# Conv b's taps behind a third of a slot, the root steps over two stages, and the third group's z gates in one slot

## The chip, the cores and the metric

The kernel runs on one core of a Trainium2 chip. The core has a matrix engine (TensorE, PE in the profile), a vector engine (VectorE, DVE), a scalar engine (ScalarE, ACT), a general engine (GpSimd, POOL) and a queue that only issues transfers (SyncE, SP). Each engine takes its instructions strictly in the order in which the program lists them, so an instruction that waits holds back everything listed behind it on its engine. The metric is the device time of one execution, in microseconds (us).

## The reference

One encoder layer is computed for a prompt of 1,024 tokens and a sample of 32 tokens; both are held together as 1,056 columns. A combined input projection of the 1,024 model features gives all branch inputs: a GLU pair and a gate for branch A, and z, x, B, C and dt for branch B, and three merge gates. In short:

```python
u = a_val * sigmoid(a_glu);  u = causal_dwconv31(u)            # conv a
out_a = (silu(layer_norm(u)) * silu(a_gate)) @ w_a_out
xbc = silu(causal_dwconv4(xbc))                                # conv b: 4 taps, 3,072 channels
xs, B, C = split(xbc);  dt = softplus(dt_raw + dt_bias)
y = ssd_scan(xs, dt, -exp(a_log), B, C, h0) + d_skip * xs      # 4 groups, state carried over the tokens
g = y * silu(z);  g = g * rsqrt(mean(g*g over a group) + eps)  # gated RMS norm, 4 groups
out_b = (g * gnorm_w) @ w_b_out
merged = sigmoid(g_a) * out_a + sigmoid(g_b) * out_b
x_new = layer_norm(alpha * x + merged @ w_out + sigmoid(g_p) * (p @ w_ple))
```

The kernel also returns the last rows of both convolutions and the final state of the scan.

## The kernel before

Channels lie on the 128 partitions, tokens along the free dimension. Every large product is done as three products of a high and a low part, so each weight tile is split by ScalarE (high part) and VectorE (low part, `wlo`).

**Slots.** The program is a list of slots written out by hand; a slot s is one or two output tiles of a product on TensorE. Slots 1 to 30 (`pair_slot`) compute pairs of tiles of the input projection. Slots 31 to 58 (S_CL on, the list `CLASSIC`) compute the 28 remaining tiles singly: z tiles, and for each of the scan's groups 1 to 3 the tiles B, C and four x tiles. Slots 59 to 70 are three quarters of the product of branch B, slots 71 to 78 branch A, 79 to 82 the last quarter, and then comes the output product. A single tile is 72 matmuls of 352 columns, in three token groups of 24, each evicted from PSUM by ScalarE (`evac`); three PSUM banks are used in turn.

**Stages of a slot** (`slot`, lines 314 to 351). Side work is put on a slot under a stage's name with `at(s, stage, fn)`. The stages run in this order: `ld0`, `ld`, `st`, `d0`, the split of the next weight tile, `a0`, `d1`; then the first token group; then `a1`; the second group; then `pm` and `a2`; the third group; then `d2`, `run_fill`, `pe` and `end`. Since each engine has its own queue, a stage says where in each engine's list the work stands.

**The scan** (`ssd_group`). Group g handles one chunk of 128 tokens per slot, from slots 32, 41, 50 and 59 on, nine chunks each. In the slot of a chunk: the decay tile L is loaded and computed on ScalarE (`decay`, `a2`), and TensorE transposes x and B at `pe`. One slot later: `prep` on VectorE (`a0`: two products into M and X, the mask, and L times it), `pe_o` on TensorE (`a1`: output from the carried state; it needs the PSUM bank of y free), `carry` on VectorE (`a2`: scales the carried state and y in PSUM), and `pe_d` on TensorE (`pe`: adds the chunk's own part into y and S, so it needs `carry` done). Two slots later: `update` (`d0`): ScalarE copies the state, and four VectorE operations read y out of PSUM. So TensorE's `pe_o` in a slot waits for `update` of the same slot, and `pe_d` at its end waits for `carry`.

**Conv b** (`conv_b`, lines 1147 to 1180). For the tile of slot s: `tap0` on ScalarE at slot s+1, `a0`; three taps on VectorE at s+1, `d2`, behind all else; SiLU on ScalarE first of all in slot s+2's `a0`. Tiles of slots 33 to 38, 42 to 47 and 52 to 57 are of this kind, so their taps stand in slots 34 to 39, 43 to 48 and 53 to 58.

**Conv a and the fill.** Conv a's 31 taps are a queue (`fill`) from which `run_fill` takes taps at a slot's end while a sum of estimated VectorE nanoseconds (`dve[0]`) is below a limit. The three taps of conv b also let up to two fills in between them. What is left at slot 37 is emptied there (`ca_flush`).

**z gates and roots** (`z_tile`, `rstd_chain`). For z tile j of group g with gate slot s: SiLU (if it comes from a pair slot) at `a1`, the gate product on VectorE at `d2` of s, its square on ScalarE at `a0` of s+1 and the sum over the four tiles on VectorE at `a1` of s+1. The group's last tile starts the root: column sums on TensorE at the end of s+1 (`stats`), the row copied by ScalarE at s+2 `a0`, moved through DRAM into 96 partitions (`move_row`, `d1`), square root and Newton step at s+2 `d2` (`root`: a square root on ScalarE and six small VectorE operations), and its store at s+2 `end`. The same chain serves conv a's layer norm with s = 53. The z gates of group 0 stand in slots 42 and 43, of group 1 in 51 and 52, of group 2 in 60 and 61, of group 3 in 71 and 72, two tiles in each.

Loads are issued from SP in the program's order, and from slot 31 on stores from POOL; both queues wait in place for what an entry needs. Buffers are handed out in the order in which the program frees them.

Of the kernel before, what the change touches and what calls it, by code (L numbers as in the profile page):

```python
# [36 lines left out]
F32 = mybir.dt.float32  # L37
# [4 lines left out]
P = 128  # L42
# [7 lines left out]
KA, KB = 31, 4  # L50
# [49 lines left out]
S_CL = 1 + len(PAIRS)  # L100
# [36 lines left out]
def emit(nc, tc, I, O, ctx):  # L137
    cpool = ctx.enter_context(tc.tile_pool(name="const", bufs=1))
# [35 lines left out]
    dve = [0.0]  # L174
# [15 lines left out]
    def tsc(out, a, s1, s2, op0, op1=None):  # L190
        dve[0] += 150 + 0.58 * width(out)
        if op1 is None:
            nc.vector.tensor_scalar(out, a, s1, None, op0)
        else:
            nc.vector.tensor_scalar(out, a, s1, s2, op0, op1)

    def act(out, a, f=AF.Copy, **kw):
        nc.scalar.activation(out, a, f, **kw)  # L198
# [21 lines left out]
    decb = cpool.tile([P, 32, 9], F32, name="decb")  # L220
    wsum = cpool.tile([P, 16], F32, name="wsum")
    small = cpool.tile([P, 64], F32, name="small")
    root_t = cpool.tile([P, 66], F32, name="root_t")
    nc.gpsimd.memset(ones, 1.0)
    nc.gpsimd.memset(epsb, EPS)
    nc.gpsimd.memset(ident, 0.0)
# [25 lines left out]
    busy = defaultdict(list)  # L252
    fill = deque()
    BREAK = object()

    def at(s, stage, fn, *a):
        todo[(s, stage)].append((fn, a))
# [6 lines left out]
    def run_fill(limit):  # L264
        while fill and dve[0] < limit:
            it = fill.popleft()
            if it is BREAK:
                break
            it()
# [44 lines left out]
    def slot(s, nm, nk, rhs, evac):  # L314

        dve_slot(11500.0 + sum(busy[s]))
        run(s, "ld0")
        w_load(s + 2)
        run(s, "ld")
        run(s, "st")  # L320
        run(s, "d0")
        w_split(s + 1)
        run(s, "a0")
        run(s, "d1")
        ws = wsplit.pop(s)
        if isinstance(ws, list):
            W = lambda q, i: ws[i // 4][q][:, i % 4 * P:i % 4 * P + P]
        else:
            W = lambda q, i: ws[q][:, i * P:i * P + P]
        spread = todo.pop((s, "dx"), [])  # L330
        n = 0
        for mi in range(nm):
            for g, (c0, c1) in enumerate(GR):
                ps = psum(bank())
                for k in range(nk):
                    xh, xl = rhs[k]
                    i = mi * nk + k
                    three(ps[:, :GN], W(0, i), W(1, i), xh[:, c0:c1], xl[:, c0:c1], k == 0, k == nk - 1)
                evac(mi, g, ps[:, :GN])
                for fn, a in spread[len(spread) * n // (3 * nm):len(spread) * (n + 1) // (3 * nm)]:  # L340
                    fn(*a)
                n += 1
                if n == nm:
                    run(s, "a1")
                elif n == 2 * nm:
                    run(s, "pm")
                    run(s, "a2")
        run(s, "d2")
        run_fill(11000.0 + sum(busy[s]))
        run(s, "pe")  # L350
        run(s, "end")

# [23 lines left out]
    def rstd_chain(get_v, scale, s, done):  # L376


        q = {}
        i = rows[0]  # L380
        rows[0] += 2
        o = 11 * 3 * (i // 2 % 2)
        sm = lambda k: root_t[:96, o + RC * k:o + RC * k + RC]

        def stats():
            q["v"] = get_v()
            q["ps"] = rows_pe(q["v"])

        def row():
            rows_copy(q["ps"], q["v"])  # L390

        def root():
            act(sm(1), sm(0), AF.Sqrt, bias=epsb[:96], scale=scale)
            tsc(sm(0), sm(0), scale, EPS, ALU.mult, ALU.add)
            nc.vector.reciprocal(sm(1), sm(1))
            newton(sm(1), sm(0), sm(2))

        def move_row():
            store(d_row[i:i + 1, :], q["v"][0:1, :])
            load(sm(0), d_row[i].rearrange("(p c) -> p c", p=96))  # L400
            tput(q["v"])

        def move_root():
            store(d_row[i + 1].rearrange("(p c) -> p c", p=96), sm(1))
            done(i + 1)

        at(s + 1, "pe", stats)
        at(s + 2, "a0", row)
        at(s + 2, "d1", move_row)
        at(s + 2, "d2", root)  # L410
        at(s + 2, "end", move_root)

    H = 32

# [722 lines left out]
    XSs, BCs, sgs, zst = {}, {}, {}, {}  # L1137
# [9 lines left out]
    def conv_b(ct, vin, s, done, stage="d2"):  # L1147

        acc = {}

        def tap0():
            acc[0] = tget((P, WB), F32, "cb")
            act(acc[0], vin[:, 0:WB], AF.Identity, bias=col(C_CBB + ct), scale=col(C_CBW + ct * KB))

        def tap(j):
            stt(acc[0], vin[:, j:j + WB], col(C_CBW + ct * KB + j), acc[0], ALU.mult, ALU.add)

        def out():
            store(O["conv_b"][ct * P:(ct + 1) * P, 0, :], vin[:, TP:TP + LB])
            store(O["conv_b"][ct * P:(ct + 1) * P, 1, :], vin[:, NT + LB:NT + 2 * LB], vin)  # L1160

        def silu():
            t = acc[0]
            act(t[:, :TP], t[:, :TP], AF.Silu)
            act(t[:, TP:NT], t[:, WB - TS:], AF.Silu)
            done(t)

        at(s + 1, "a0", tap0)

        def taps():  # L1170
            for j in range(1, KB):
                tap(j)
                if stage == "d2" and j < KB - 1 and fill and fill[0] is not BREAK and dve[0] < 9000.0:
                    fill.popleft()()
        at(s + 1, stage, taps)
        at(s + 2, "st", out)
        if s + 2 < S_CL:
            at(s + 2, "a2", silu)
        else:
            todo[(s + 2, "a0")].insert(0, (silu, ()))  # L1180

    def z_tile(g, j, zt, s):


        q = {"z": zt}

        def away():
            store(d_z[4 * g + j], zt, zt)

        def back():  # L1190
            q["z"] = tget(name="zt")
            load(q["z"], d_z[4 * g + j])

        def late_silu():
            act(q["z"], q["z"], AF.Silu)

        if s - cur[0] > 4:
            at(cur[0] + 1, "st", away)
            at(s, "ld", back)
        if cur[0] < S_CL:  # L1200
            at(s, "a1", late_silu)

        def gate():
            x = XSs[4 * g + j][:, :NT]
            tt(x, x, q["z"], ALU.mult)

        def square():
            act(q["z"], XSs[4 * g + j][:, :NT], AF.Square)

        def add():  # L1210
            if j == 0:
                zst[g] = q["z"]
            else:
                tt(zst[g], zst[g], q["z"], ALU.add)
                tput(q["z"])

        at(s, "d2", gate)
        at(s + 1, "a0", square)
        at(s + 1, "a1", add)

        def spill():
            store(d_yn[4 * g + j], XSs[4 * g + j][:, :NT], XSs[4 * g + j])

        at(s + 1, "a1", spill)
        if j == 3:
            rstd_chain(lambda: zst[g], 1.0 / 512, s, lambda i: yrow.update({g: i}))
# [310 lines left out]
    SSD0 = [S_CL + i for i in (1, 10, 19, 28)]  # L1537
# [67 lines left out]
    for i, (ta, tb) in enumerate(PAIRS):  # L1605
        s = i + 1
        cur[0] = s
        ba, bb = BIAS(2 * i), BIAS(2 * i + 1)
        (kind, n, _), (kb, nb, _) = ta, tb
        if kind == "glu":  # L1610
            sg = tget(name="sg")
            u = uin_tile(n)
            ca[n] = (u, sg)
            oa, ob = plain(sg), padded(u, LA, TP + 2 * LA)
            at(s + 1, "a0", lambda sg=sg: act(sg, sg, AF.Sigmoid))
            conv_a_ready(n, s + 1)
        elif kind in ("gate", "z"):
            ga, gb = tget(name="ga"), tget(name="gb")
            oa, ob = plain(ga), plain(gb)
            if kind == "z":  # L1620
                for z_, m in ((ga, n), (gb, nb)):
                    z_tile(m // 4, m % 4, z_, SSD0[m // 4] + (12 if m > 11 else 10) + m % 4 // 2)
            elif 8 <= n < 16:
                base_tiles(s, (ga, gb), (n - 8, nb - 8))
            else:
                at(s + 1, "st", gate_spill, ga, n)
                at(s + 1, "st", gate_spill, gb, nb)
        else:
            va, fa = vin_tile(kind, n)
            vb, fb = vin_tile(kb, nb)  # L1630
            oa, ob = padded(va, LB, TP + 2 * LB), padded(vb, LB, TP + 2 * LB)
            last = s == len(PAIRS)
            fa(s, *(() if last else ("a1",)))
            fb(s, *(() if last else ("a2",)))
        pair_slot(s, oa, ob, ba, bb)
# [14 lines left out]
    for ti, (kind, n, _) in enumerate(CLASSIC):  # L1650
# [7 lines left out]
        if kind == "z":  # L1658
# [2 lines left out]
            def evac(mi, g, ps, zt=zt, bias=bias):  # L1661
                act(zt[:, GR[g][0]:GR[g][1]], ps, AF.Silu, bias=bias)
            g_ = n // 4
            z_tile(g_, n % 4, zt, max(s + 1, SSD0[g_] + 10 + n % 4 // 2))
        elif kind == "glu":
            sg = sgs[n] = tget(name="sg")

# [249 lines left out]
```

## Time and profile before

| | |
|---|---|
| median of 3 runs | 1540.13 us (1538.54 to 1540.93) |
| the profiled execution | 1544.62 us; span 1542.8 us from the first to the last instruction |
| mean granted clock of TensorE | 0.989 |
| busy: TensorE, VectorE, ScalarE, GpSimd | 97%, 78%, 56%, 19% of the span |
| a slot with a chunk of the scan and no wait | 15.35 us (slot 47 from 913.80 to 929.15) |

Times in the trace are counted from the first instruction. Slots can be read off TensorE's rows: slot 31 begins at 659.45, slot 40 at 792.93, slot 50 at 964.17, slot 60 at 1127.19. A row of the timeline has its start, its length, the engine, the line, the operation, what it writes and reads, shapes, a count, and in brackets how long the engine had been idle before it and whose end released it. Names are the program's tiles with the buffer's letter: `cb` is a conv b tile, `vin` its input, `hT` the state of the scan, `L`, `M`, `X` the scan's operands, `cao` and `cae` conv a's two sums, `zt` a z tile, `root_t` the cells of the root, `cw` a weight tile that is being centred.

### The profile page before, as it was taken

The page shows a single profiled execution, that of the slowest core. Times are in us where ns is not written, and L with a number is a line of the kernel's source. Part 1 is how long each engine was busy: PE and PEld are TensorE (multiplying, and loading weights), DVE is VectorE, ACT ScalarE, POOL GpSimd, SP SyncE. Part 2 cuts the span into 40 slices and gives each one's busy share as a digit, 9 for nine tenths or more (in the row PEclk, how much of TensorE's full clock was granted, in tenths as well). Part 3 has the DMA queues.
Part 4 walks back from the last instruction along what each step waited for, and adds up shares of the span by engine and source line. Part 5 has one row for each costly group of instructions (what it writes and reads, how often), then busy time and mean ns, then how long its engine had stood idle before and what let it go on. Part 6 is the DMA issues. An engine that isn't in the chain of part 4 may idle for free.

```text
span 1542.8 us, 27648 instructions
## 1 busy us (share of the span) xinstructions
PE 1502.1 (97%) x10967; PEld 1455.5 (94%) x10967; DVE 1203.4 (78%) x1650; ACT 862.8 (56%) x1490; POOL 290.4 (19%) x445
## 2 busy tenths in 40 slices
PE   8999999999999999999999899998999999999997
PEld 7999999999999999998999788988988899999997
DVE  6669898989889899899875867666866887768554
ACT  7644635444444344576775677676877466634343
POOL 1343333333333333100001111001000000000000
PEclk9999999999999999999999999999999999999998
DMA  9987797988877686453548875764293545654132
GB/s 325 235 216 212 175 246 201 263 222 235 223 196 196 170 207 163 109 172 98 141 137 281 288 231 160 239 147 125 83 288 113 174 177 203 223 224 167 44 96 73
DMA packets 156306, 288.43 MB, mean 187 GB/s; under 512 B 26992, under 2 KB 83344, under 8 KB 156176
## 3 DMA queue, kind: packets, MB, share of 16 engines
q1 hardware_dynamic: 111936, 176.06, 36.0%
q0 software_dynamic: 44240, 110.61, 28.7%
q8 instruction: 86, 1.41, 0.4%
q14 instruction: 44, 0.36, 0.1%
HBM read 226.14 MB, written 60.46 MB: 186 GB/s over the span
## 4 chain that ended last, share of the span: by engine, by line
PE 84%; DVE 5%; ACT 4%; DMA 4%; issue 2%; SPq 1%; POOL 0%; ACTq 0%; DVEq 0%; POOLq 0%
PE ps L211 83%; SPq L201 1%; DVE cb_z L188 1%; ACT L198 1%; DMA cw_z<-in_wo 1%; DMA yraw_t<-d_yn 1%; PE ps L1058 1%; DMA cb_z<-d_base 1%; ACT L_t L198 1%; ACT L_z L198 1%; DMA w<-in_wdt 0%; DVE cae_u L188 0%; DMA E<-d_expa 0%; DMA s<-in_w 0%; DVE yraw_t L188 0%
## 5 line engine op out<-in xcount | busy, mean ns | idle before, releaser
L500 POOL DMA_DIRECT2D s<-in_w x150 | 132.3, 924 | 275.4 <-DMA s<-in_w 203.2
L188 DVE SCALAR_TENSOR_TENSOR cae_u<-uin_u,par,cae_u 128x1086 f32<-128x1086 f32 x120 | 161.2, 1343 | 0.0
L188 DVE SCALAR_TENSOR_TENSOR cao_u<-uin_u,par,cao_u 128x1086 f32<-128x1086 f32 x112 | 150.5, 1344 | 0.0
L184 DVE TENSOR_TENSOR wlo<-wraw,whi 128x1024 fp32r<-128x1024 f32 x53 | 64.8, 1223 | 44.4 <-ACT whi L198 44.3
L198 ACT ACT_TABLE_LOAD x73 | 93.7, 1283 | 2.9 <-DMA zt_t<-d_z 0.8
L198 ACT ACTIVATE whi<-wraw 128x1024 fp32r<-128x1024 f32 x53 | 55.9, 1054 | 42.1 <-PE ps L211 41.4
L495 POOL DMA_DIRECT2D r<-in_w x85 | 63.4, 799 | 28.2 <-DVE w_0l L184 20.3
L211 PE MATMUL ps<-t3h,w_4l 128*128 128x264 f32 x240 | 68.7, 286 | 0.0
L211 PE MATMUL ps<-n2h,w_2h 128*128 128x264 f32 x240 | 68.6, 286 | 0.0
L211 PE MATMUL ps<-t3l,w_4h 128*128 128x264 f32 x240 | 68.4, 285 | 0.0
L211 PE MATMUL ps<-t4h,w_6h 128*128 128x264 f32 x240 | 68.4, 285 | 0.0
L211 PE MATMUL ps<-n2l,w_2h 128*128 128x264 f32 x240 | 68.3, 285 | 0.0
L211 PE MATMUL ps<-t3h,w_4h 128*128 128x264 f32 x240 | 68.3, 285 | 0.0
L211 PE MATMUL ps<-n2h,w_2l 128*128 128x264 f32 x240 | 68.2, 284 | 0.0
L495 POOL DMA_DIRECT2D s<-in_w x84 | 48.2, 575 | 106.1 <-issue 28.2
L211 PE MATMUL ps<-t4l,w_6h 128*128 128x264 f32 x240 | 68.1, 284 | 0.0
L211 PE MATMUL ps<-t4h,w_6l 128*128 128x264 f32 x240 | 67.9, 283 | 0.0
L198 ACT ACTIVATE gb_t<-ps,par 128x528 f32<-128x528 f32 x32 | 22.5, 702 | 71.7 <-PE ps L211 67.6
L198 ACT ACTIVATE ga_t<-ps,par 128x528 f32<-128x528 f32 x38 | 26.7, 702 | 63.8 <-PE ps L211 63.8
L198 ACT ACTIVATE ps<-ps 128x528 f32<-128x528 f32 x28 | 16.7, 595 | 62.3 <-PE ps L211 62.3
L211 PEld LDWEIGHTS ps<-t3h,w_4h 128*128 128x128 f32 x240 | 45.3, 189 | 0.0
L211 PEld LDWEIGHTS ps<-n2l,w_2h 128*128 128x128 f32 x240 | 45.3, 189 | 0.0
(1174 smaller groups left out, 6062.0 us busy)
## 6 DMA issues: line engine op xcount, KB each, us to landing
s<-in_w POOLq DMA_DIRECT2D x234, 256.0 KB, 4.8
r<-in_w POOLq DMA_DIRECT2D x85, 256.0 KB, 5.1
wraw<-in_w SPq DMA_DIRECT2D x27, 512.0 KB, 8.2
wraw<-in_wb SPq DMA_DIRECT2D x16, 512.0 KB, 3.7
E<-d_expa SPq DMA_DIRECT2D x56, 128.0 KB, 7.9
d_gate<-ga_t SPq DMA_DIRECT2D x12, 528.0 KB, 6.3
L_z<-d_accp SPq DMA_DIRECT2D x12, 512.0 KB, 6.7
d_gate<-gb_t SPq DMA_DIRECT2D x10, 528.0 KB, 7.3
```

The source lines that it names most:

```text
L184: nc.vector.tensor_tensor(out, a, b, op)
L188: nc.vector.scalar_tensor_tensor(out, a, s, b, op0, op1)
L198: nc.scalar.activation(out, a, f, **kw)
L201: nc.sync.dma_start(dst, src)
L211: nc.tensor.matmul(out, l, r, start=start, stop=stop, skip_group_check=more)
L495: (nc.gpsimd if cur[0] else nc.sync).dma_start(t, pw_src(i, PARTS[n][0]))
L500: nc.gpsimd.dma_start(pr[i, n], pw_src(i, (PARTS[n] + ("12",))[k]), accum_op=ALU.add)
L1058: nc.tensor.transpose(pX[:nt, j * P:(j + 1) * P], XS[j][:, sl], ident)
```

## The change

Three edits go together.

1. **Taps.** For the tiles of slots 31 and later, the three conv b taps move from `d2` to `a1` of the same slot, and no fill is put between them. The limit of the fill in `slot` goes from 11,000 to 10,000.
2. **Roots.** The square root moves from `d2` of s+2 to `a0` of s+3, the VectorE steps become a function of their own (`steps`) at `a1` of s+3, and the store goes from `end` of s+2 to `a2` of s+3. Since two chains may now overlap, there are three sets of cells (99 columns).
3. **z gates.** All four z gates of group 2 stand in slot 60; the two that come from pair slots had been in slot 61. Their loads, SiLUs, squares and sums move with them by one slot, and so does the group's root chain, whose s becomes 60. The sum takes whichever tile comes first as its start.

```diff
-    root_t = cpool.tile([P, 66], F32, name="root_t")
+    root_t = cpool.tile([P, 99], F32, name="root_t")
@@ slot
-        run_fill(11000.0 + sum(busy[s]))
+        run_fill(10000.0 + sum(busy[s]))
@@ rstd_chain
-        o = 11 * 3 * (i // 2 % 2)
+        o = 11 * 3 * (i // 2 % 3)
...
         def root():
             act(sm(1), sm(0), AF.Sqrt, bias=epsb[:96], scale=scale)
+
+        def steps():
             tsc(sm(0), sm(0), scale, EPS, ALU.mult, ALU.add)
             nc.vector.reciprocal(sm(1), sm(1))
             newton(sm(1), sm(0), sm(2))
...
-        at(s + 2, "d2", root)
-        at(s + 2, "end", move_root)
+        at(s + 3, "a0", root)
+        at(s + 3, "a1", steps)
+        at(s + 3, "a2", move_root)
@@ conv_b
-                if stage == "d2" and j < KB - 1 and fill and fill[0] is not BREAK and dve[0] < 9000.0:
+                if s < S_CL and stage == "d2" and j < KB - 1 and fill and fill[0] is not BREAK and dve[0] < 9000.0:
                     fill.popleft()()
-        at(s + 1, stage, taps)
+        at(s + 1, "a1" if s >= S_CL else stage, taps)
@@ z_tile
-            if j == 0:
+            if g not in zst:
                 zst[g] = q["z"]
@@ the slots of the gates
-                    z_tile(m // 4, m % 4, z_, SSD0[m // 4] + (12 if m > 11 else 10) + m % 4 // 2)
+                    z_tile(m // 4, m % 4, z_, SSD0[m // 4] + (10, 10, 10, 12)[m // 4] + (m // 4 != 2) * (m % 4 // 2))
...
-            z_tile(g_, n % 4, zt, max(s + 1, SSD0[g_] + 10 + n % 4 // 2))
+            z_tile(g_, n % 4, zt, max(s + 1, SSD0[g_] + 10 + (g_ != 2) * (n % 4 // 2)))
```

## The prediction

> **What bounds the kernel now.** I read the page first. TensorE is busy nearly all the time, so time can be gained only where TensorE stands still or runs slowly.
>
> ```profile
> PE 1502.1 (97%) x10967; PEld 1455.5 (94%) x10967; DVE 1203.4 (78%) x1650; ACT 862.8 (56%) x1490; POOL 290.4 (19%) x445
> ```
>
> Next, the view of waits for TensorE alone: who was waited for, total, times, longest (us).
>
> ```profile
> PE ps L211 <- DVE cb_t L188: 11.6, 3, 6.0
> PE ps L211 <- DVE cb_z L188: 6.4, 3, 3.2
> ...
> PE ps L211 <- DVE cb_y L188: 2.0, 1, 2.0
> ```
>
> The three `cb` rows are 20.0 us in seven waits. Each is the scan's `pe_o` waiting for `update`, because VectorE came late into the slot. The view by windows of single slots (length, busy time of each engine, granted clock, DMA share, GB/s) places them: slots 34, 44, 46, an undisturbed one (47), 48, 55, 56, 60 and 64.
>
> ```profile
> 697.74:716.20 18.46, 16.47 (x115) 14.49 (x113) 18.39 (x22) 8.86 (x19) 0.74 (x2) 1.00 0.32 70
> 854.09:878.11 24.02, 18.00 (x114) 16.14 (x112) 23.25 (x29) 14.85 (x26) 5.40 (x10) 0.86 0.86 266
> 893.47:913.80 20.33, 17.14 (x108) 15.98 (x107) 17.51 (x27) 13.97 (x25) 5.97 (x11) 0.92 0.96 292
> 913.80:929.15 15.35, 15.35 (x108) 14.44 (x107) 10.40 (x16) 12.58 (x23) 1.07 (x2) 1.00 0.76 235
> 929.15:948.70 19.55, 17.18 (x109) 16.00 (x107) 18.61 (x25) 12.65 (x21) 3.26 (x6) 0.91 0.65 184
> 1041.52:1060.99 19.47, 17.15 (x108) 15.98 (x107) 10.87 (x21) 13.58 (x26) 2.13 (x4) 0.91 0.38 78
> 1060.99:1081.33 20.34, 17.16 (x108) 15.98 (x107) 15.86 (x29) 13.00 (x24) 3.07 (x6) 0.92 0.52 165
> 1127.19:1143.09 15.90, 14.96 (x101) 13.45 (x99) 9.80 (x13) 11.63 (x24) 1.62 (x3) 1.00 0.95 270
> 1190.48:1211.00 20.52, 17.32 (x108) 15.86 (x107) 14.11 (x30) 13.27 (x21) 0.53 (x1) 0.92 0.61 201
> ```
>
> Length less TensorE's busy time is its idle time: 2.0, 6.0, 3.2, 0, 2.4, 2.3, 3.2, 0.9 and 3.2 us. Where it was 2.3 us or more the granted clock fell to 0.86 to 0.92, and the same work took 1.8 us longer (17.14 against 15.35 in slot 46; 17.18, 17.15, 17.16 alike); at 2.0 us (slot 34) the clock stayed at 1.00. So a wait costs itself, and 1.8 us more from somewhere between 2.0 and 2.3 us on.
>
> The Trainium skill (TensorE: Matmul & The Clock Gate, Part 1) has the clock halved after an idle window of about 3.4 us; the trace disagrees, 2.3 us were enough here. By the page the new wait in slot 58 below would cost 1.8 us less, and the sum would be 1523 instead of 1525 us.
>
> **Part 1a, taps: slots 43 and 44.** The timeline there (VectorE, then ScalarE, then TensorE):
>
> ```profile
> 847.98 0.69 DVE L184 TENSOR_TENSOR ps<-ps,E 128x512 f32<-128x512 f32 x1
> 853.82 1.23 DVE L184 TENSOR_TENSOR cw_z<-cw_z,wsum 128x1024 f32<-128x1024 f32 x1 [5.15 <-DMA cw_z<-in_wo]
> 855.54 1.23 DVE L184 TENSOR_TENSOR cw_z<-cw_z,wsum 128x1024 f32<-128x1024 f32 x1 [0.49 <-DMA cw_z<-in_wo]
> ...
> 859.02 4.03 DVE L188 SCALAR_TENSOR_TENSOR cb_z<-vin_z,par,cb_z 128x1059 f32<-128x1059 f32 x3
> ...
> 870.94 0.69 DVE L184 TENSOR_TENSOR ps<-ps,E 128x512 f32<-128x512 f32 x1
> 847.94 1.27 ACT L198 ACTIVATE cb_z<-vin_z,par 128x1059 f32<-128x1059 f32 x1 [5.20 <-DMA out_ssm<-hT_z]
> 851.41 1.09 PE L211 MATMUL ps<-L_u,X 128*64 128x128 f32 x16
> 864.24 2.05 PE L211 MATMUL ps<-cb_t,hT_u 128*128 128x128 f32 x8 [6.02 <-DVE cb_t L188]
> 874.54 1.09 PE L211 MATMUL ps<-L_t,X 128*64 128x128 f32 x16
> ```
>
> VectorE finishes `carry` at 848.7, idles until 853.8 for a load, and the taps (4.03) come last, so `update` ends only at 864.2, where `pe_o` starts after 6.0 us. At `a1` the taps fill that hole, but stand ahead of `carry`. Tap 0 ends at 849.2 (its buffer waits for a store), so the taps end at 853.2 and `carry` (two operations of 0.69, started 0.6 apart: 1.3) at 854.5: `pe_d`, at 851.4 before, now waits 3.2 us. The rest of the slot starts 0.7 later, of which the second load's 0.5 is made up, so without the taps `update` ends at 864.2 less 4.0 plus 0.2, 860.4. From it to the end of slot 44's `carry` are 7.4 us (864.2 to 871.6), with the taps now inside 11.4: `pe_d` of slot 44 starts at 871.8 instead of 874.5. **Gain 2.8**; bounds: 0 if loads hold VectorE up, 7.8 if tap 0 comes early.
>
> **1b, slot 48.** The same lateness, with no such hole to lose: the taps leave the tail, `update` comes 4.0 earlier, more than the 2.4 waited. The slot returns to 15.35: **gain 4.2**, bounds 0 (loads then end last) and 4.2.
>
> **1c, new waits for `carry`.** In a quiet slot `carry` ends long before `pe_d`. Slot 38:
>
> ```profile
> 770.52 0.69 DVE L184 TENSOR_TENSOR ps<-ps,E 128x512 f32<-128x512 f32 x1
> 774.91 1.09 PE L211 MATMUL ps<-L_z,X 128*64 128x128 f32 x16
> ```
>
> 771.2 plus 4.0 is 775.2, 0.3 late. Doing this for all eighteen tap slots gives 0.3 in 38 and 39, 0.2 in 53, 0.4 in 57, nothing where no other work stands before `carry`: **loss 1.2** (0 to 3). The exception is slot 58, where branch B's first operands stand there too:
>
> ```profile
> 1104.87 1.31 DVE L188 SCALAR_TENSOR_TENSOR yraw_z<-yraw_z,par,yrb_u 128x1056 f32<-128x1056 f32 x1
> ...
> 1107.88 0.70 DVE L184 TENSOR_TENSOR ps<-ps,E 128x512 f32<-128x512 f32 x1
> 1109.35 1.09 PE L211 MATMUL ps<-L_y,X 128*64 128x128 f32 x16
> ```
>
> The taps go behind the 1104.87 row; `carry` moves from 1108.6 to 1112.6 and `pe_d` from 1109.4 (1109.8 after slot 57's 0.4): 2.9 us, over the bound of the clock: **loss 4.7** (1.8 to 6).
>
> **1d, the fill.** Followed by the cost lines 182 to 195, the lower limit drops one conv a tap (1.34) from slot 32 and adds one in 36; 33 to 35 keep eight, three and three. VectorE enters slot 34 1.26 us earlier, which comes off the 2.0 waited there: **gain 1.2** (0 to 2.0). The final addition moves to slot 37, whose VectorE has room.
>
> **Part 2, roots.** The square root stood behind the last eviction, so VectorE waited for it to the slot's end with the taps behind it. First the view of `root_t` for VectorE, then rows of slot 54 and ScalarE:
>
> ```profile
>   ACT root_t L198: 29.4, 4
> 1041.71 0.17 DVE L195 TENSOR_SCALAR root_t<-root_t 96x11 f32<-96x11 f32 x1 [10.66 <-ACT root_t L198]
> 1040.08 1.28 ACT L198 ACT_TABLE_LOAD   x1
> 1041.38 0.30 ACT L198 ACTIVATE root_t<-root_t,epsb 96x11 f32<-96x11 f32 x1
> 781.20 1.26 ACT L198 ACTIVATE cb_t<-vin_z,par 128x1059 f32<-128x1059 f32 x1
> ```
>
> These waits (slots 45, 54, 55, 63) make the long slots 46, 55, 56 and 64. VectorE now works on and does the steps (1.1) after `prep`. What is late next: the table load and root (1.6) go ahead of tap 0 on ScalarE. In slot 39 (start 777.58) tap 0 ends 4.9 into the slot; here 6.5 to 7.6, so `carry` (4.0 plus 1.3 behind it) ends 11.8 to 13.2 in, against `pe_d` at 12.7 (851.41 less 838.73): 0.3 lost in 46, none in 55, 0.5 in 56. **Gain** 4.7 + 4.1 + 4.4 = **13.2** (9 to 14.4), and in slot 64, without taps, 20.52 less 15.4: **5.1** (2 to 5.2). Behind the root on POOL stood the stores of the next slot; they leave earlier. The stores' readers follow slots later, and group 2's chain starts a slot sooner. The two roots of group 3 and the wider cells cost nothing: slots 72 to 75 have no wait.
>
> The Trainium skill (ScalarE: Activation LUTs, What ACT_TABLE_LOAD costs) adds a drain of about 1.38 us to each table load. The trace does not show it here: the root starts 0.02 us after its load. With it the three slots would lose some 4 us more: 1529.
>
> **Part 3, z gates.** Slot 60 gets two more loads, two SiLUs, two gates; slot 61 the squares and sums that 62 had. What that does is read from ScalarE's and TensorE's rows of slot 60:
>
> ```profile
> 1136.79 1.09 ACT L198 ACTIVATE y5h_t<-yraw_t 128x1056 fp32r<-128x1056 f32 x1 [4.23 <-DVE yraw_t L188]
> 1138.28 0.43 PE L211 MATMUL ps<-y0l_t,whi 128*128 128x352 f32 x1 [0.44 <-ACT acc_t L198]
> ```
>
> The load and the SiLUs themselves, in slot 61:
>
> ```profile
> 1150.43 1.28 ACT L198 ACT_TABLE_LOAD   x1
> 1151.73 2.06 ACT L198 ACTIVATE zt_t<-zt_t 128x1056 f32<-128x1056 f32 x2
> ```
>
> In slot 60 they come behind `y5h`, which is late already, and ahead of the eviction for which TensorE waits at 1138.28. Load and SiLUs (3.3) make 0.4 into 3.7 us, and the clock 1.8 more; slot 61 loses 0.4 to four squares and gains back its SiLUs' place. **Loss 5.5** (0 if ScalarE gets to them early, up to 8 as the two loads join a slot whose DMA share is 0.95).
>
> **The sum.** 2.8 + 4.2 + 13.2 + 5.1 + 1.2 = 26.5 gained, 1.2 + 4.7 + 5.5 = 11.4 lost, net 15.1. The profiled execution took 1544.62 us (span 1542.8), 4.5 above the median; 1544.6 less 15.1 is 1529.5, against the median of 1540.1 **1525 us**.
>
> **Rivals.** (A) The new waits of slots 58 and 60 don't arise or stay under the clock's bound: 1540.1 less 25.3 is 1515. For it: slot 58's is only 0.6 over the bound; against: both follow from fixed queue orders. (B) Loads end last once the waits are gone: the gains of 44, 46 and 48 (11.7) don't come, 1537. For it: DMA shares 0.86 and 0.96 there; against: in 47 the loads kept pace, and POOL's stores spread better. (C) Slower: tap 0 comes so late that in all of 43 to 48 and 53 to 58 `pe_d` waits for `carry` over the bound, which begins where tap 0 ends later than 9.6 us into the slot (12.7 + 2.2 less 5.3). Each costs 4.1: eleven slots beside 58 take 45 from a net 15: 1570. Slot 43 shows it can happen (10.5); the others' 4.9 speaks against. (D) The change only shifts waits: VectorE, 17.5 to 23 us busy in 44, 46 and 48, stays the bound and TensorE stands as long at `pe_d` as before at `pe_o`: 1540. Against: its long idle before the roots. (E) The table load holds ScalarE twice its 1.28: 1.3 more in 46, 55 and 56, 1529.
>
> **Chances.** Forecast 0.44, A 0.20, B 0.14, C 0.08, D 0.08, E 0.06. About 0.2% (3 us) is what a measurement can tell. Faster: forecast, A, E and most of B, 0.83; same 0.09 (D and the edge of B); slower 0.08. The forecast's own range is 1520 to 1530; for 8 in 10 it reaches to A's lower end (1511) and to B (1537).
>
> **What would show it.** Right: no wait at `pe_o` over 1 us after slot 34; slots 46, 48, 55 and 64 between 15.3 and 16 with clock 1.00; VectorE's waits for the square root gone; a `pe_d` waiting for VectorE 3 us in 43 and 58; a wait near 3.7 for ScalarE's eviction in 60. Wrong: waits for loads at `d2` in 46 to 48 that move into the next `pe_o` (B), `pe_d` waits in 45 to 47 (C), or clean slots 58 and 60 (A).

## The result and the profile after

The changed kernel takes **1528.74 us** (median of four runs, 1527.30 to 1530.08) against 1540.53 of the kernel before (four runs, 1538.54 to 1545.02). The ratio is 0.9918 with a 95% interval of 0.9893 to 0.9944. Beside a later set of runs, on the chip of the last experiment, it was 0.9913 (0.9887 to 0.9939). The forecast was 1525, or a ratio of 0.990, in a range of 1511 to 1537.

The view of waits for TensorE in the changed kernel (who was waited for, total, times, longest) answers to the one of before. All `cb` rows but one are gone; in their place stand waits for `carry` (`ps L184`) and for one eviction by ScalarE.

```profile
PE ps L211 <- DVE ps L184: 8.8, 8, 4.0
...
PE ps L211 <- ACT acc_t L198: 2.7, 1, 2.7
...
PE ps L211 <- DVE cb_y L188: 1.6, 1, 1.6
```

To see where the time went I cut both traces at the slots' first matmuls. First some stretches of the kernel before that the prediction does not show: slot 43, slot 58, slots 60 to 62 together, slots 64 and 65 together (length, busy time of TensorE, its weight loads, VectorE, ScalarE and GpSimd, granted clock, DMA share, GB/s).

```profile
838.73:854.09 15.36, 15.36 (x108) 14.41 (x107) 9.33 (x16) 9.41 (x20) 1.60 (x3) 1.00 1.05 355
1096.68:1112.15 15.47, 15.47 (x108) 14.22 (x106) 14.84 (x19) 14.16 (x25) 1.08 (x2) 1.00 0.23 69
1127.19:1175.21 48.02, 46.76 (x317) 42.33 (x315) 32.99 (x44) 37.75 (x71) 2.69 (x5) 1.00 0.68 203
1190.48:1227.00 36.52, 32.87 (x214) 30.21 (x212) 27.76 (x51) 21.23 (x36) 0.53 (x1) 0.95 0.59 183
```

The changed kernel: slots 34, 43, 44, 46, 48, then 55 and 56 together, 58, 60, then 60 to 62 and 64 to 65 together.

```profile
695.22:713.39 18.17, 16.53 (x115) 14.48 (x113) 18.07 (x22) 8.84 (x19) 0.73 (x2) 1.00 0.18 44
836.52:857.80 21.28, 17.29 (x109) 15.36 (x107) 17.46 (x22) 9.91 (x20) 3.66 (x7) 0.92 0.81 281
857.80:874.41 16.61, 16.31 (x115) 14.64 (x113) 16.01 (x25) 14.44 (x25) 2.52 (x6) 1.00 1.02 288
889.76:905.24 15.48, 15.42 (x109) 14.44 (x107) 12.85 (x21) 14.16 (x25) 2.06 (x4) 1.00 0.92 259
920.56:936.32 15.76, 15.66 (x108) 14.41 (x107) 15.66 (x21) 12.73 (x21) 3.34 (x7) 1.00 0.84 234
1029.17:1060.35 31.18, 30.75 (x213) 28.84 (x212) 22.40 (x42) 26.87 (x49) 4.48 (x9) 1.00 0.54 149
1075.99:1095.90 19.91, 17.07 (x109) 14.73 (x107) 15.57 (x21) 15.65 (x28) 1.28 (x3) 0.92 0.27 74
1110.97:1129.75 18.78, 16.11 (x101) 14.91 (x99) 12.22 (x15) 14.53 (x27) 2.67 (x5) 0.91 1.03 314
1110.97:1161.83 50.86, 47.71 (x316) 43.79 (x315) 33.26 (x44) 36.94 (x72) 3.18 (x6) 0.97 0.65 198
1177.14:1210.72 33.58, 31.11 (x213) 28.68 (x212) 25.99 (x42) 19.64 (x34) 0.00 (x0) 1.00 0.53 161
```

Set against each other, in us gained (a minus is a loss):

| place | predicted | measured |
|---|---|---|
| 43 and 44, taps | 2.8 | 1.5 (39.38 to 37.89) |
| 48, taps | 4.2 | 3.8 |
| 38, 39, 53, 57, waits for `carry` | -1.2 | -0.9 |
| 58, wait for `carry` | -4.7 | -4.4 |
| 34, fill | 1.2 | 0.3 |
| 46, 55, 56, roots | 13.2 | 13.5 (60.14 to 46.66) |
| 64 (and 65), root | 5.1 | 2.9 |
| 60 to 62, z gates | -5.5 | -2.8 |
| sum, slots 31 to 70 | 15.1 | 13.9 |

The profiled execution after took 1527.30 us, 17.3 less than the one before. Besides the 13.9, 2.5 are in the stretch up to slot 31 (659.45 to 656.97), whose work the change leaves alone, and 0.9 behind slot 70. In the traces of the other kernels below slot 31 begins between 656.23 and 662.88, so I take both as scatter between single executions. The medians differ by less, by 11.8.

The timeline of slot 43 shows the new wait as it was drawn: tap 0 late behind a store (ScalarE), then the taps, `carry` behind them (VectorE), `pe_d` (TensorE).

```profile
846.87 1.28 ACT L198 ACTIVATE cb_z<-vin_z,par 128x1059 f32<-128x1059 f32 x1 [6.13 <-DMA out_ssm<-hT_z]
848.18 4.04 DVE L188 SCALAR_TENSOR_TENSOR cb_z<-vin_z,par,cb_z 128x1059 f32<-128x1059 f32 x3 [2.71 <-ACT cb_z L198]
852.13 0.69 DVE L184 TENSOR_TENSOR ps<-hT_u,decb 128x512 f32<-128x512 f32 x1
...
853.49 0.84 PE L211 MATMUL ps<-L_u,X 128*64 128x128 f32 x6 [3.99 <-DVE ps L184]
```

And slot 60: table load and SiLUs in front of the eviction for which TensorE waits.

```profile
1119.80 1.28 ACT L198 ACT_TABLE_LOAD   x1
1121.09 2.06 ACT L198 ACTIVATE zt_t<-zt_t 128x1056 f32<-128x1056 f32 x2
1123.55 0.66 PE L211 MATMUL ps<-y0l_t,whi 128*128 128x352 f32 x1 [2.67 <-ACT acc_t L198]
```

So the ledger was right in its sum and in its largest lines. Part of that is luck: slot 64, slots 43 and 44, the fill and slot 48 together fell 4.8 us short, but the z gates cost 2.7 less than forecast, and the other lines gave 0.9 more. The experiments show one thing more that was not right: whose gain the 13.5 us are.

### The profile page after: what moved, and what is told of

Its sections match the earlier page's. It is cut to its first block, busy times and chain, and to the rows that moved or that the text cites. A ratio compares the mean times of both kernels' runs of the same rounds, so it can differ in the third digit from the quotient of the medians.

```text
span 1525.6 us, 27668 instructions
## 1 busy us (share of the span) xinstructions
PE 1492.4 (98%) x10967; PEld 1445.1 (95%) x10967; DVE 1204.4 (79%) x1650; ACT 863.4 (57%) x1490; POOL 289.6 (19%) x445
## 4 chain that ended last, share of the span: by engine, by line
PE 79%; DVE 5%; ACT 5%; DMA 5%; issue 4%; SPq 1%; POOL 0%; ACTq 0%; DVEq 0%; POOLq 0%
PE ps L211 78%; DMA s<-in_w 2%; SPq L201 1%; DMA cb_u<-d_base 1%; ACT L198 1%; PE ps L1061 1%; ACT L_z L198 1%; DMA E<-d_expa 1%; DMA yraw_t<-d_yn 1%; DVE ps L184 1%; DVE cb_y L188 1%; DMA w<-in_wdt 1%; ACT whi L198 1%; DVE cao_u L188 1%; ACT L_t L198 0%
## 5 line engine op out<-in xcount | busy, mean ns | idle before, releaser
L184 DVE TENSOR_TENSOR wlo<-wraw,whi 128x1024 fp32r<-128x1024 f32 x53 | 64.9, 1224 | 52.1 <-ACT whi L198 51.9
L211 PEld LDWEIGHTS ps<-t4l,w_6h 128*128 128x128 f32 x240 | 45.1, 188 | 0.7 <-ACT gb_u L198 0.5
L211 PEld LDWEIGHTS ps<-n2h,w_2l 128*128 128x128 f32 x240 | 45.3, 189 | 0.0
```

The source lines that it names most:

```text
L184: nc.vector.tensor_tensor(out, a, b, op)
L211: nc.tensor.matmul(out, l, r, start=start, stop=stop, skip_group_check=more)
```

## The experiments

Between slots 31 and 70 the profiled kernels took: before 636.65, changed 622.77. The same stretch is given for each experiment, as it leaves out most of the scatter; the ratios are of whole times, to the kernel before on the same chip.

### The taps alone

Edit 1 with the fill limit, nothing else:

```diff
+        at(s + 1, "a1" if s >= S_CL else stage, taps)
         ...
         at(s + 2, "d2", root)          # as before
```

> Edit 1 alone (taps at a1, the fill limit); roots and z gates as before. Theory 1, separate gains (as the prediction's ledger adds them): only slots 43 and 44 together (1.5 by the changed kernel's trace), 48 (3.8) and 34 (0.3) gain, 38, 39, 57 (0.9) and 58 (4.4) lose; the stalls of 46, 55, 56 stay because the square root still ends at the slot's end: about 1540 us, no change. Theory 2, one cause seen twice: in 46, 55 and 56 the late update is root wait plus taps; with the taps gone from the tail the steps end about 1.0 us and update about 2.3 us into the slot, before pe_o at 4.0, so the 13.5 us of these three slots come from this edit alone: about 1527 us, and only slot 64 keeps its 20.5 us.

1532.63 us, ratio 0.9917 (0.9885 to 0.9949); 624.45 between the slots. Theory 2 holds, though its 1527 was reckoned from 1540 for the kernel before, which stood at 1543.76 on this chip. VectorE still stands 5.92 us for the square root until after slot 55 has begun (1035.04), and yet the slot is as short as an undisturbed one (timeline of VectorE, then the window of slot 55):

```profile
1035.24 0.17 DVE L195 TENSOR_SCALAR root_t<-root_t 96x11 f32<-96x11 f32 x1 [5.92 <-ACT root_t L198]
```

```profile
1035.04:1050.39 15.35, 15.35 (x109) 14.44 (x107) 10.96 (x21) 13.58 (x26) 2.13 (x4) 1.00 0.24 58
```

The steps that follow take 1.1 and `update` 1.1, so `update` is done before `pe_o` can start. Slots 46 and 56 fell to 15.72 and 15.34 in the same way. Slot 64, which has no taps, stayed at 20.41.

### The roots alone

Edit 2 without the other two. Group 2's chain is left at its old place, since one slot later its root would be written after the load that reads it:

```diff
+        if s == 61:
+            at(s + 2, "d2", root); at(s + 2, "d2", steps); at(s + 2, "end", move_root)
+        else:
+            at(s + 3, "a0", root); at(s + 3, "a1", steps); at(s + 3, "a2", move_root)
         ...
         at(s + 1, stage, taps)         # as before
```

> Edit 2 alone, except that group 2's chain keeps its old place (moved, its root would be written after the load that reads it). Taps and z gates as before. Both theories: the root waits of 46, 55, 56 go, 13.2 us; 44 (6.0 wait) and 48 (2.4 wait) and 64 stay: about 1527 us. It tells theory 1 from 2 together with taps_only and no_gates: if both single edits give about 13 us and both together no more than one of them plus the 2 to 6 us of 43, 44, 48 and 58, the two edits buy the same waits.

1528.44 us, ratio 0.9890 (0.9857 to 0.9922); 621.99 between the slots. Slots 46, 55 and 56 are at 15.33 to 15.35, and 53 to 58 are all clean, without the waits for `carry`. What the taps at the tail cost stays in slots 44 and 48 (windows of 46, 44 and 48):

```profile
893.32:908.66 15.34, 15.34 (x108) 14.43 (x107) 12.86 (x24) 14.15 (x25) 3.24 (x6) 1.00 0.84 270
853.64:877.96 24.32, 19.16 (x114) 17.30 (x112) 23.13 (x30) 17.28 (x31) 5.38 (x10) 0.86 0.88 275
924.01:943.16 19.15, 17.17 (x109) 16.00 (x107) 17.32 (x21) 12.64 (x21) 2.93 (x6) 0.91 0.70 186
```

This edit alone is as good as the whole change.

### Taps and roots without the z gates

```diff
-            if g not in zst:
+            if j == 0:
         ...
         # group 2's z gates in 60 and 61, its chain at the old place
```

> The changed kernel without edit 3; group 2's z gates in slots 60 and 61 and its chain at the old place. My theory: slots 60 to 62 lose their 2.8 us (18.78 + 16.76 + 15.32 back to 15.90 + 15.91 + 16.21), slots 64 and 65 take 2.9 us back (16.77 + 16.82 to 20.52 + 16.00), net 0: 1528.7 us. Rival of the ledger as predicted: z gates cost 5.5 and the root of group 2 gains 5.1, 1528.3. Rival that the gates are what costs and 64 is cured by the other edits: 1524 to 1526.

1529.02 us, ratio 0.9892 (0.9858 to 0.9925); 621.10 between the slots. With the two kernels above it settles the attribution: 12.2 us for the taps alone, 14.7 for the roots alone, 15.6 for both. **The two edits buy the same waits**; on top of the roots the taps bring 0.9 us, within scatter. The z gates are the trade that was forecast: 60 to 62 take 47.81 instead of 50.86, and slot 64 takes 18.95 instead of 16.76. Moving the gates is the price for moving the root of group 2 (the load that reads it comes in slot 64), and the trade about cancels: without it the stretch between the slots is 1.7 us shorter in single executions, and the intervals of the two ratios overlap widely (0.9858 to 0.9925 without it, 0.9893 to 0.9944 with it).

```profile
1075.98:1094.36 18.38, 15.53 (x108) 14.22 (x106) 15.57 (x21) 15.07 (x28) 1.07 (x2) 1.00 0.24 69
1172.54:1191.49 18.95, 15.78 (x108) 14.31 (x107) 14.10 (x30) 12.45 (x20) 0.53 (x1) 1.00 0.60 187
```

These two rows, slots 58 and 64, also hold something not expected: both have a wait over 2.2 us and a clock of 1.00. It is taken up below.

### The taps behind `carry`

```diff
-        at(s + 1, "a1" if s >= S_CL else stage, taps)
+        if s >= S_CL:
+            todo[(s + 1, "d2")].insert(0, (taps, ()))
```

> The changed kernel with the taps first in d2, behind carry and ahead of the other d2 work. Theory: every pe_d wait for carry goes (slots 38, 39, 56, 57: 0.3 each; 58: 2.84 and its slow clock, 4.4; 43: 3.99 and its slow clock, 5.9), but in 43 VectorE then ends late itself: taps from 848.2 to 852.2, the centring and gates behind, so that update of slot 44 ends some 2.2 us after pe_o could start, and 2.2 to 4.0 come back there. Net 7.5 to 9.3: 1519 to 1521 us. Rival (VectorE isn't the bound of 43): 11.5, 1517. Rival (waits only shift, D): 58's and 43's waits come back in full at pe_o: 1528.

1526.28 us, ratio 0.9874 (0.9844 to 0.9904); 621.61 between the slots, 1.2 less than the changed kernel instead of 7.5 or more. Slots 43 and 58 are clean (15.37, 15.47) and 43 and 44 together take 33.64 instead of 37.89. But 48 is back at 19.48, and slots 59 to 61 got worse: what slot 58 gains they lose. Slot 59's window, VectorE's rows and the queue's rows say why:

```profile
1090.41:1108.31 17.90, 15.66 (x107) 14.41 (x106) 9.42 (x19) 8.58 (x21) 0.54 (x1) 0.98 0.81 265
```

```profile
1090.69 1.25 DVE L184 TENSOR_TENSOR y3l_u<-yraw_z,y3h_u 128x1056 fp32r<-128x1056 f32 x1
1103.36 1.32 DVE L188 SCALAR_TENSOR_TENSOR yraw_t<-yraw_t,par,yrb_y 128x1056 f32<-128x1056 f32 x1 [7.52 <-DMA yraw_t<-d_yn]
```

```profile
1093.51 1.48 SPq L201 DMA_DIRECT2D yraw_t<-d_yn  x2
```

The low part `y3l` comes behind the taps now; the loads of the next y tiles are issued 1.6 us after its end; and VectorE stands 7.5 us for them, ahead of `carry`. That the loads wait for `y3l` is in the view of waits for the queue, from 1085 to 1096 us:

```profile
SPq L201 <- DVE y3l_u L184: 14.4, 1, 14.4
```

In this kernel the waits of slot 58 shift, as rival D of the prediction had it; those of 43 do not.

### A mixture by slot

Roots, no z gates, taps at `a1` in slots 44 to 48 alone and first in `d2` elsewhere:

```diff
+        if 44 <= s + 1 <= 48:
+            at(s + 1, "a1", taps)
+        elif s >= S_CL:
+            todo[(s + 1, "d2")].insert(0, (taps, ()))
```

> Edit 2 with group 2's chain at its old place, no edit 3, and the taps at a1 in slots 44 to 48 alone, elsewhere from 31 on first in d2. Theory (each stretch bound by its own late link, stretches independent): slots 43 and 44 as in taps_behind (33.6 us), 45 to 48 as in the changed kernel (61.9), 58 to 62 as in roots_only (77.5 against 85.8), 38, 39, 56 and 57 at 15.35, 64 and 65 as in roots_only (36.7 against 33.6): 10.8 us less than the changed kernel between slots 31 and 71, about 1518 us. Rival (waits only shift along VectorE's queue, as 58's did into 59 to 61 in taps_behind): no better than roots_only, 1526 to 1529.

1526.46 us, ratio 0.9878 (0.9853 to 0.9902); 621.43 between the slots. The theory of independent stretches falls: slot 44 took 21.14 (a wait of 2.05 for `update`, one of 0.97 for `carry`, and a clock of 0.92), 48 took 20.05, and 59 took 17.17, again standing for the y tile. The rival's time came.

### The mixture with group 2's root ahead of the third token group

```diff
-            at(s + 2, "d2", root)
-            at(s + 2, "d2", steps)
+            at(s + 2, "pm", root)
+            todo[(s + 2, "d2")].insert(0, (steps, ()))
```

> As mix, but group 2's square root stands before the third token group of slot 63 (its row had landed 7.8 us into that slot, the third group starts at 9.9) and its VectorE steps first in d2. Theory: VectorE no longer waits to the slot's end, slot 64 falls from 19 to 20.5 to about 16.8 as in the changed kernel: 2 to 4 us under mix, about 1515. Rival: the table load and the root stand ahead of the decay and the third group's eviction on ScalarE, which is as late as VectorE was: same as mix.

1523.75 us, ratio 0.9871 (0.9848 to 0.9894); 617.41 between the slots. Slot 64 fell to 16.75, as with the moved gates: the stall of slot 64 can be removed without moving them. Slot 59 was 18.82.

### The SiLUs behind the second token group

The changed kernel with one stage name altered:

```diff
-            at(s, "a1", late_silu)
+            at(s, "pm" if g == 2 else "a1", late_silu)
```

> The changed kernel with group 2's two SiLUs behind the second token group instead of the first. Theory of the prediction (slot 60's wait is the eviction behind table load and SiLUs): the 2.67 wait and its slow clock go, slot 60 falls from 18.8 to about 15.0, 1525 us. Rival (the slot is held by late loads: in taps_behind VectorE stood 7.5 us in slot 59 for a y tile): the y tile's high part and the eviction stay late, 60 and 61 keep most of their loss, 1528.

1528.67 us, ratio 0.9902 (0.9878 to 0.9926); 623.37 between the slots. Both expectations are half right. Slot 60's wait is gone, so it was the eviction behind load and SiLUs; but slot 61 pays for it (windows of both slots, then TensorE's row):

```profile
1112.71:1127.16 14.45, 14.45 (x100) 13.53 (x99) 9.00 (x10) 10.24 (x21) 1.08 (x2) 1.00 1.02 295
1127.16:1148.00 20.84, 16.82 (x115) 14.45 (x113) 15.49 (x22) 17.12 (x32) 1.60 (x3) 1.00 0.59 196
```

```profile
1130.55 0.43 PE L211 MATMUL ps<-y0l_t,whi 128*128 128x352 f32 x1 [1.21 <-ACT acc_t L198]
```

The SiLUs now stand ahead of the decay, and ScalarE reaches the evictions late in the slot behind.

### The same wait in six slots

Eight extra products on a scratch tile ahead of `carry` in slots 38, 39, 46, 48, 53 and 57 of the changed kernel:

```diff
             def carry(i=i, nt=nt):
+                for _ in range(8 if s0 + i + 1 in (38, 39, 46, 48, 53, 57) else 0):
+                    tt(pad, pad, pad, ALU.mult)
```

> The changed kernel with the same eight extra VectorE products on a scratch tile ahead of carry in slots 38, 39, 46, 48, 53 and 57, so that TensorE waits about 2.4 to 2.8 us at pe_d in each. Theory of the prediction (a wait over about 2.2 us always costs 1.8 us more by a lower clock): all six slots take their wait plus 1.8, some 26 us in all. Rival (it depends on where the wait falls, not on its length alone, as the 2.85 us wait of slot 58 cost nothing more in no_gates): some of the six pay, others don't, 16 to 24 us.

One execution, 1557.14 us. The windows of slots 38, 39, 46 and 48, and the waits at `pe_d` in 38 and 39:

```profile
758.96:780.61 21.65, 17.86 (x108) 16.11 (x107) 15.90 (x24) 12.21 (x23) 2.16 (x4) 0.87 0.54 169
780.61:799.19 18.58, 15.94 (x108) 14.95 (x107) 15.89 (x24) 12.34 (x21) 0.00 (x0) 0.97 0.13 41
899.88:921.35 21.47, 17.86 (x108) 16.11 (x107) 17.94 (x32) 14.78 (x26) 3.41 (x7) 0.85 0.72 209
936.86:956.21 19.35, 17.06 (x108) 15.30 (x107) 17.60 (x29) 14.10 (x24) 2.89 (x6) 0.91 0.66 173
```

```profile
775.49 0.91 PE L211 MATMUL ps<-L_z,X 128*64 128x128 f32 x6 [3.79 <-DVE ps L184]
796.51 1.09 PE L211 MATMUL ps<-L_z,X 128*64 128x128 f32 x16 [2.64 <-DVE ps L184]
```

The waits came out longer than meant, 2.3 to 3.8 us. What a slot took beyond 15.35 us (16.24 in 53) and its wait was 2.5 in 38 and 46, 0.6 in 39, 1.7 in 48, and 1.7 in 53 and 57 too. A fixed price falls; the last section shows where the 2.5 and the 0.6 come from. The sum, about 30 us over the undisturbed slots, doesn't tell the two apart, as the waits missed their size; the single slots do.

### What frees the y tiles

As the mixture with the earlier root, but the taps last in `d2` again from slot 53 on, behind `y3l`, and first in `d2` in 44 too:

```diff
+        if 45 <= s + 1 <= 48:
+            at(s + 1, "a1", taps)
+        elif s >= S_CL and s + 1 <= 44:
+            todo[(s + 1, "d2")].insert(0, (taps, ()))
+        else:
+            at(s + 1, stage, taps)
```

> As mix_root, but in slots 53 to 58 the taps stand last in d2 as in the kernel before, and in 43 and 44 first in d2. Theory: in mix and mix_root the taps of slot 58 stood ahead of the low part y3l, whose end frees the buffer of the next y tile, so that its load came late and VectorE stood 7 us in slot 59; with y3l ahead of the taps slots 59 and 60 return to 15.05 and 14.9 (17.2 to 18.8 and 15.2 to 16.2 in the two mixes), and 44 pays no carry wait (20.3 to 18.3): 3 to 6 us under mix_root. Rival (59 is held by other loads, whatever frees the buffer): as mix_root.

**1520.39 us**, ratio 0.9849 (0.9819 to 0.9879); 611.70 between the slots. Counted from the slot's start, `y3l` comes 4.0 us earlier than in the kernel with the taps behind `carry`, the loads are issued as much earlier, and VectorE's stand in 59 is halved, which is short enough for `carry`. Slot 59 is 3.8 us shorter than in the mixture with the earlier root, and the whole stretch 5.7, as expected:

```profile
853.04:871.91 18.87, 16.48 (x115) 14.62 (x113) 18.66 (x23) 16.38 (x28) 3.22 (x6) 1.00 1.02 290
1090.80:1105.87 15.07, 15.07 (x108) 14.05 (x106) 9.46 (x19) 9.58 (x21) 0.54 (x1) 1.00 0.94 321
```

```profile
1087.12 1.25 DVE L184 TENSOR_TENSOR y3l_u<-yraw_z,y3h_u 128x1056 fp32r<-128x1056 f32 x1
...
1099.90 1.32 DVE L188 SCALAR_TENSOR_TENSOR yraw_t<-yraw_t,par,yrb_y 128x1056 f32<-128x1056 f32 x1 [3.68 <-DMA yraw_t<-d_yn]
```

The queue waits for `y3l` here too, but ends that wait earlier in the slot (waits from 1085 to 1096 us):

```profile
SPq L201 <- DVE y3l_u L184: 12.8, 1, 12.8
```

It beats the kernel before, and its interval lies below that of the changed kernel beside it. Slots 44 and 48 (18.87 and 18.19) still hold a wait each.

### The changed kernel beside it

> The changed kernel once more, unaltered, beside mix_loads: 12 us under the kernel before; where mix_loads gains what its theory says, it is 8 to 10 us under this one.

1531.11 us, ratio 0.9913 (0.9887 to 0.9939), 10.7 us above the last kernel on the same chip. Its profiled execution had its long waits at the same places (43, 58 and 60) and two more of 1.1 and 1.2 us, in slots 43 and 48; slot 43 took 22.87 instead of 21.28.

## Why the prediction was right, and where it was not

- **Roots in 46, 55 and 56: the size right, the credit not.** 13.2 predicted, 13.5 measured, and the detail held: in slot 46 `carry` ends 12.7 us into the slot and costs 0.1. But the step "VectorE now works on and does the steps after `prep`" was not needed for it. Update was late by root and taps together, and taking away either is enough. The ledger came out right only because it counted these three slots under one edit; costed edit by edit, its lines for the taps alone come to 2.3 us (2.8 + 4.2 + 1.2 - 1.2 - 4.7) where 12.2 were measured. This was in the rows: 10.66 us of VectorE idle, then 1.1 of steps, then 4.0 of taps, against a `pe_o` 4.0 us into the slot.
- **Taps in 43 and 44**: the mechanism held (tap 0 late, taps ahead of `carry`), the size was off. `pe_d` waited 3.99 instead of 3.2, because tap 0 ended 11.6 us into the slot instead of 10.5, and the slow clock, which I had left out here, took 1.9 more. TensorE had no wait left at slot 44's `pe_o`, so 44 gained 7.4, 43 lost 5.9, and 1.5 of 2.8 came.
- **Slot 58**: 4.4 for 4.7, wait 2.84 for 2.9.
- **Fill**: one tap (1.26) less before slot 34 brought 0.3. The step that failed is that what VectorE no longer does comes off the wait whole; VectorE reached slot 33's weight split before ScalarE had its high part and stood 0.75:

```profile
685.82 1.23 DVE L184 TENSOR_TENSOR wlo<-wraw,whi 128x1024 fp32r<-128x1024 f32 x1 [0.75 <-ACT whi L198]
```

- **Slot 64**: 5.1 predicted, 3.8 there and 0.8 lost in 65. I had let it fall to 15.4, as if nothing were late behind the root. VectorE's weight split waits for ScalarE there too, so that its additions from PSUM come 1.2 us late in both slots:

```profile
1179.70 1.23 DVE L184 TENSOR_TENSOR wlo<-wraw,whi 128x1024 fp32r<-128x1024 f32 x1 [2.41 <-ACT whi L198]
```

- **z gates**: the wait was forecast at 3.7 and was 2.67; with the clock, 60 to 62 lost 2.8 of 5.5, as `y5h` came earlier in its slot than before (7.7 us into it instead of 9.6), and slot 62 gained 0.9.
- **The clock**: "a wait costs itself, and 1.8 us more from somewhere between 2.0 and 2.3 us on" is wrong as a rule: the 1.8 us depend on where the wait falls (last section). In this kernel it served, since the waits of 43, 58 and 60 all paid.
- **Rivals**: B did not come in the changed kernel; loads became the last link as soon as slot 58 ran faster (the taps behind `carry`). C's long waits came only in 43 and 58. D is nearly what the taps show on top of the roots: against the roots alone, slots 43, 44 and 48 gain 4.9 (59.43 to 54.52), and 58 and the short waits for `carry` take most of it back.

## What to carry to other kernels

Before adding up gains, ask of each stall how much of its lateness each edit removes: where two pieces of work make one operation late, and it is late by less than either takes (here 2.3 to 3.2 us, against 4.0 of taps), the first edit takes the whole gain and the second brings nothing. An operation moved ahead of another on an in-order engine also moves whatever the other one frees; here a 1.25 us subtraction that released a buffer decided a load, and the load a slot. The order that is best in one slot is not best in the next, so choose it by slot, from what stands last there.

## What the runs showed of the hardware

The same wait does not cost the same clock. Slot 64 waited 2.26 us in the kernel before and ran at 0.92, and 2.25 us in the kernel without the z gates and ran at 1.00; slot 58 waited 2.84 and 2.85 us and took 19.91 and 18.38 us. TensorE's rows with slot 64's wait, of the kernel before and of the one without the z gates:

```profile
1200.82 0.43 PE L211 MATMUL ps<-y4l_t,whi 128*128 128x352 f32 x1 [2.26 <-DVE acc_t L184]
```

```profile
1182.87 0.43 PE L211 MATMUL ps<-y4l_t,whi 128*128 128x352 f32 x1 [2.25 <-DVE acc_t L184]
```

What tells them apart is in the traces' clock. Between slots 31 and 70 it is 0.50 only in stretches of 3.41 us, or of two such steps, and in one trace all these stretches start a whole number of steps of 3.41 us apart: in the kernel before at 860.67, 901.63, 935.77, 1048.41, 1068.89 and 1202.01, which is 12, 10, 33, 6 and 39 steps. Cut on that grid, the steps around slot 64's wait, of the kernel before and of the one without the z gates (whose grid hangs on its only such stretch, from 854.22), are as follows; the clock is the last number but two:

```profile
1198.59:1202.01 3.42, 1.19 (x7) 1.20 (x8) 3.03 (x5) 1.65 (x2) 0.00 (x0) 1.00 0.92 314
1202.01:1205.42 3.41, 3.41 (x14) 3.41 (x13) 1.65 (x3) 0.60 (x1) 0.00 (x0) 0.50 0.84 225
```

```profile
1178.49:1181.91 3.42, 2.13 (x14) 1.84 (x13) 3.39 (x6) 0.00 (x0) 0.00 (x0) 1.00 0.71 177
1181.91:1185.32 3.41, 2.45 (x15) 2.45 (x16) 2.00 (x5) 2.25 (x2) 0.00 (x0) 1.00 0.98 352
```

In the first, one step holds 2.2 us of idle time and the next runs at half rate; in the second the wait is split over two steps, 1.3 and 1.0, and both steps and the one behind run at full rate. Slot 58's 2.84 us lay 0.4 and 2.4, its 2.85 us 1.0 and 1.8. Over slots 31 to 70 of all twelve traces, a step at full rate in which TensorE stood 1.9 us or more was followed by one at half rate in all 31 cases; of the 51 with 1.0 to 1.9 us, two were (1.84 us in the kernel with the same wait in six slots, and 1.44 us in slot 59 with the taps behind `carry`). So a wait's length alone decides little here: one of 3.27 us, split 1.8 and 1.5, cost no clock (slot 60 with the taps behind `carry`), and one of 1.98 us in a single step did (slot 48 with the roots alone, 0.91). Before slot 31 and behind slot 70 a few steps with 1.1 to 1.9 us of idle time were followed by half rate too, so idle time is not the whole condition, and what it is stays open.

A step of 3.41 us at half rate costs half of the time that TensorE works in it, at most 1.7 us. A half-rate step that still held 0.5 us or more of a wait was followed by another, in all seven cases; one with 0.3 or less by none. That gives the odd prices above: slot 38 lost 2.5 us because two such steps in a row ended its wait and followed it, and the 0.6 us of slot 39 are the end of slot 38's second step (781.78, with slot 39 from 780.61), so its own wait of 2.64 us cost no clock.

The Trainium skill (TensorE: Matmul & The Clock Gate, Part 1) has the gate watch windows of about 3.4 us that run freely and don't start with the work; the steps of 3.41 us agree with it. That 1.9 us of idle time in a step suffice does not agree with an idle window as a condition, and the prediction went by a wait's length alone, not by where it falls.

Part of the scatter between executions is this chance. In the two profiled executions of the changed kernel slot 43's long wait was 3.99 and 3.69 us; one half-rate step followed it in the first, two in the second, and they cost the slot 1.9 and 2.7 us. Eleven executions of the kernel before on one chip ran from 1537.75 us at a mean clock of 0.994 to 1551.37 at 0.988.
